# Three merge-gate tiles on blocks 0 and 1 between the halves of the first convolved tiles, and the first root written in front

## The chip, the cores and the metric

The kernel runs on one core of one Trainium2 chip. The metric is the device time of one execution, in microseconds (us). Before the change three runs took 3191.61, 3194.91 and 3195.35 us; the median is 3194.91 us. One more execution was taken by the hardware profiler, and all rows quoted below come from it.

## The reference

Two equal layers of an encoder over 2048 tokens with 1024 channels, in float32, and an RMSNorm at the end. One layer, cut to what matters here:

```python
h = rms_norm(x, norm_w)                      # over the 1024 channels of a token
proj = h @ w_in                              # 1024 -> 5648 columns
qkv, z_a, a_lg, b_lg, cf_val, cf_glu, z_b, gate_lg = split(proj)
qkv = silu(depthwise_conv(qkv, width 5))     # branch A: gated DeltaNet, 4 heads
o = gated_delta(q, k, v, g, beta)            # chunked scans, forward and backward
y_a = (rms(o) * dn_norm_w * silu(z_a)) @ w_dn_out
u = depthwise_conv(cf_val * sigmoid(cf_glu), width 31) + cf_conv_b   # branch B
y_b = (silu(layer_norm(u)) * silu(z_b)) @ w_cf_out
gate = sigmoid(gate_lg + gate_b)             # 2 x 1024 columns: the merge gates
x = x + (gate[0] * y_a + gate[1] * y_b) @ w_out
```

## The kernel before

**Tiling.** Channels lie on the partitions, tokens on the free axis. The 2048 tokens are four *blocks* of 512 (blocks 0 and 1 are the first *half*). The normalised input of a block is held as `h` in two parts, a rounded one and its remainder (`split`, L156: ScalarE rounds, VectorE subtracts), and so is every weight tile (`whi`, `wlo`). One *dense tile*, 128 output channels by one block, is 8 steps over the input channels with three matmuls each (L174 whi by hi, L175 whi by lo, L176 wlo by hi), 24 matmuls of 128x512. `weight` (L160) loads a tile in two halves through the raw buffers `wraw` and splits both. There are two buffers each for `wraw`, `whi` and `wlo`.

**Order of the program.** Engines run their queues in order. A scheduler puts the instructions of the first stages into each queue, from the order in which the code issues them, the free buffers, and its own estimates; in the recurrence (`delta`) the written order is kept. The stages of a layer are: per head `conv_tiles` for k and q, then v, then the two conformer projections and two activated tiles; then `gates(0)`, the 16 merge-gate tiles on blocks 0 and 1 (32 dense tiles); then `delta`, the scans; then `merge`.

**Work on the side.** VectorE's long work, the 31-tap convolutions, the triangular solves and the layer norms of the conformer branch, sits in the list `back`, and `pump` releases some of it after every dense tile (L177 to L183). `delta` has short matmuls with long waits between them; dense work for TensorE comes from `filler`: `gates(1)`, the 16 gate tiles on blocks 2 and 3, and then `early_merge`, which computes the branch B product for blocks 0 and 1 (operand `uop`). The filler hands out 8 steps for each of its 32 gate tiles and 4 for each of the 16 products, 320 steps in all; `delta` pulls 304 of them by the constants LEAD, STEP and TAIL, and runs what is left after its last instruction. Where `back` isn't empty after `gates(0)`, the layer pulls filler steps, 8 at a time, until it is (the `while self.back` loop at L375).

**The first normalisation** (`first_norm`, L287) is a generator that advances step by step. For each block it squares and adds up the 8 channel tiles of `x` (`sqa`; block 0 on VectorE, the others on GpSimd) and yields; then it sums over the partitions on TensorE (`token_sum`, L198, into `nv`), takes the inverse square root by nine small VectorE instructions (`rsqrt`, L187) and yields; then it spreads the root over the partitions (`dg`, L208), scales `x` (L327) and splits it into `h`, with a yield after every second channel tile. `need` and `step_lead` advance it from inside `conv_tiles`.

**The first convolved tiles** (`conv_tiles([4, 0], block)`) keep their two weight tiles over both halves. Per block they compute the small projection `wab` (16 matmuls, L408 and L409) and two dense tiles, k and q; after each half they convolve both with 5 taps (one ScalarE instruction, L551, and four VectorE taps, L553) and apply SiLU.

**The hand-over to the merge.** The last chunk pair's scans are transposed on TensorE (L1045), multiplied by the SiLU gate (L1046), stored to `og`, loaded again as `gop` and split; the first dense tiles of `merge` read `gop`.

Of the kernel before, what the change touches and what calls it, by code (L numbers as in the profile page):

```python
# [14 lines left out]
P = 128  # L15
# [4 lines left out]
KD = 8  # L20
# [5 lines left out]
R1 = 3.0  # L26
R3 = 4.5
GAP = 0
SPLIT = 247
LEAD = (8, 10, 6, 6, 6, 4)  # L30
STEP = (4, 4, 4, 4)
# [45 lines left out]
class Trunk:  # L77
# [120 lines left out]
    def token_sum(self, ps, src, n):  # L198
        for i in range(n):
            self.nc.tensor.matmul(ps[:, i:i + 1], src[:, i * P:(i + 1) * P], self.ones[:, 0:1],  # L200
                                  start=True, stop=True)

    def spread(self, ps, r, n):
        dg = self.pst.tile([P, NB], F32, tag="st", name="dg").rearrange("p (a b) -> p a b", b=P)
        for i in range(n):
            self.nc.vector.tensor_scalar(out=dg[:, i, :], in0=self.ident, scalar1=r[:, i:i + 1],
                                         scalar2=None, op0=ALU.mult)
            self.nc.tensor.matmul(ps[:, i * P:(i + 1) * P], self.ones, dg[:, i, :], start=True, stop=True)  # L208
# [39 lines left out]
    def run(self):  # L248
        tc, nc, a = self.tc, self.nc, self.a
        with tc.tile_pool(name="cst", bufs=1) as cst, \  # L250
                tc.tile_pool(name="vec", bufs=1) as self.pv, \
                tc.tile_pool(name="dsc", bufs=1) as self.pds, \
                tc.tile_pool(name="big", bufs=4) as self.pbig, \
                tc.tile_pool(name="mid", bufs=3) as self.pmid, \
                tc.tile_pool(name="hmd", bufs=5) as self.phm, \
                tc.tile_pool(name="stg", bufs=3) as self.pst, \
                tc.tile_pool(name="sml", bufs=14) as self.psm, \
                tc.tile_pool(name="wgt", bufs=2) as self.pw, \
                tc.tile_pool(name="drm", bufs=1, space=DRAM) as drm, \
                tc.tile_pool(name="pdn", bufs=3, space=PSUM) as self.ppd, \  # L260
                tc.tile_pool(name="pzz", bufs=5, space=PSUM) as self.ppz:
            con = cst.tile([P, 4, P], F32, name="con")
            nc.scalar.dma_start(con, a["consts"])
            self.ident = con[:, C_ID, :]
            self.ones = con[:, C_ONE, :]
            self.con = con
            self.sig = cst.tile([P, 1], F32, name="sig")
            nc.gpsimd.memset(self.sig[0:64], 1.0)
            nc.gpsimd.memset(self.sig[64:128], -1.0)
            self.junk = cst.tile([P, P], mybir.dt.bfloat16, name="junk")  # L270
            fnw = cst.tile([P, KD], F32, name="fnw")
            nc.scalar.dma_start(fnw, a["fnorm"])
            self.drm = drm
            xd = None
            self.vec = self.pv.tile([P, NV], F32, tag="vec", name="vec")
            nc.scalar.dma_start(self.vec, a["vecs"][0])
            self.ready = 0
            h = [None] * 4
            self.h = h
            self.scalar_weights(0)  # L280
            self.lead = self.first_norm(a)
            next(self.lead)
            xd = [a["x"][k] for k in range(KD)]
            for l in range(self.depth):
                h, xd = self.layer(l, h, xd, fnw)

    def first_norm(self, a):  # L287
        nc = self.nc
        stage = self.big([P, 2, KD, NB], F32, "x0")
        for blk in range(4):  # L290
            half, b = divmod(blk, 2)
            self.h[blk] = self.big([P, 2, KD, NB], F32R, f"h{blk}")
            hi, lo = self.h[blk][:, 0], self.h[blk][:, 1]
            src = [a["x"][k, :, blk * NB:(blk + 1) * NB] for k in range(KD)]
            if half == 0:
                x = [stage[:, b, k, :] for k in range(KD)]
            elif b == 0:
                x = self.first_tiles()
            if blk < 3:
                for k in range(KD):  # L300
                    self.load(x[k], src[k])
            acc = self.st("sqa")
            eng = nc.gpsimd if blk else nc.vector
            for k in range(KD):
                sq = self.st("sq0") if k else acc
                if blk == 3:
                    self.load(sq, src[k])
                nc.scalar.activation(sq, sq if blk == 3 else x[k], AF.Square)
                if k:
                    eng.tensor_tensor(out=acc, in0=acc, in1=sq, op=ALU.add)  # L310
            yield
            ps = self.pz()
            self.token_sum(ps, acc, 4)
            v = self.sm(4, "nv")
            r = self.sm(4, "nr")
            nc.vector.tensor_scalar(out=v, in0=ps[:, 0:4], scalar1=1.0 / D, scalar2=EPS,
                                    op0=ALU.mult, op1=ALU.add)
            self.rsqrt(r, v, 4)
            yield
            if blk == 3:  # L320
                x = self.first_tiles()
                for k in range(KD):
                    self.load(x[k], src[k])
            pr = self.pz()
            self.spread(pr, r, 4)
            for k in range(KD):
                nc.vector.scalar_tensor_tensor(out=x[k], in0=x[k], scalar=self.vec[:, V_NW + k:V_NW + k + 1], in1=pr,  # L327
                                               op0=ALU.mult, op1=ALU.mult)
                self.split(hi[:, k, :], lo[:, k, :], x[k])
                if k == KD - 1:  # L330
                    self.ready = blk + 1
                if k % 2:
                    yield
# [13 lines left out]
    def layer(self, l, h, xd, fnw):  # L347
        self.l = l
        self.h = h
        self.kq_d = self.drm.tile([NCH, P, H, 2, P], F32, name=f"kq{l}")  # L350
        self.kv_d = self.drm.tile([NCH, P, 2, H, P], F32, name=f"kv{l}")
        self.g_d = self.drm.tile([NCH, P, H, 2, P], F32, name=f"gr{l}")
        self.inv_d = self.drm.tile([H, P, 1024], F32, name=f"inv{l}")
        self.gc_d = self.drm.tile([P, P], F32, name=f"gc{l}")
        self.gs_d = self.drm.tile([P, P], F32, name=f"gs{l}")
        self.bp_d = self.drm.tile([H, 32, P], F32, name=f"bp{l}")
        self.za_d = self.drm.tile([H, P, L], F32, name=f"za{l}")
        self.zb_d = self.drm.tile([4, P, L], F32, name=f"zb{l}")
        self.cv_d = self.drm.tile([4, P, L], F32, name=f"cv{l}")
        self.u_d = self.drm.tile([4, P, L], F32, name=f"u{l}")  # L360
        self.gt_d = self.drm.tile([16, P, L], F32, name=f"gt{l}")
        self.o_d = self.drm.tile([NCH, P, H, P], F32, name=f"o{l}")
        self.og_d = self.drm.tile([H, P, L], F32, name=f"og{l}")
        for j in range(H):
            self.head(j)
            self.conformer(j)
            self.act_tile(24 + j, self.zb_d[j], AF.Silu)
            self.act_tile(12 + j, self.za_d[j], AF.Silu)
        for blk in range(4):
            self.back.append(self.conformer_norm(blk))  # L370
        self.rate = R3
        for _ in self.gates(0):
            pass
        self.fill = self.filler()
        while self.back:  # L375
            for _ in range(KD):
                next(self.fill)
        self.drain()
        self.rate = 0.0
        self.delta()  # L380
        return self.merge(l, xd, fnw)
# [124 lines left out]
    def conv_tiles(self, cols, block=None):  # L506
        nc = self.nc
        self.rate = R1
        ws = [self.weight(self.a["w_in"][self.l, c], KD) for c in cols]
        accs = []  # L510
        prev = [None] * len(cols)
        for half in range(2):
            cur = []
            for i, c in enumerate(cols):
                cur.append(self.padded(half, TAPS, prev[i], "cin") if half or not i else None)
            for b in range(2):
                blk = 2 * half + b
# [4 lines left out]
                for i, c in enumerate(cols):  # L522
                    self.step_lead(2)
                    ps = self.pd()
# [7 lines left out]
            for i, c in enumerate(cols):  # L532
# [4 lines left out]
                n = HALF - 2 if half == 0 else HALF + 2  # L537
# [248 lines left out]
        v_.tensor_tensor(out=cv, in0=cv, in1=zb, op=ALU.mult)  # L786
        self.pstore(self.u_d[:, :, sl].rearrange("j p t -> p j t"), cv)

    def gates(self, half):
        nc = self.nc  # L790
        seq = [(j, b) for j in range(16) for b in range(2)]
        if half:
            seq = seq[:28] + [(14, 0), (15, 0), (14, 1), (15, 1)]
        ws = {}
        for i, (j, b) in enumerate(seq):
# [3 lines left out]
            blk = 2 * half + b  # L799
            ps = self.pd()  # L800
# [11 lines left out]
    def delta(self):  # L812
# [240 lines left out]
        def pull(n):  # L1053
            for _ in range(n):
                if next(fill, GAP) == GAP:
                    return
# [70 lines left out]
    def filler(self):  # L1127
        wcf = self.a["w_cf"][self.l]
        u = None
        for n, v in enumerate(self.gates(1)):  # L1130
# [9 lines left out]
            if n == 31 * KD - 1:  # L1140
                ahead = self.weight(wcf[0], 4)
            if SPLIT <= n < SPLIT + 8:
                b, k = divmod(n - SPLIT, 4)
# [229 lines left out]
```

## Time and profile before

| | |
|---|---|
| median of three runs | 3194.91 us |
| the profiled execution, its own time | 3187.47 us |
| its span on the core | 3185.7 us |
| busy share of the span: TensorE, VectorE, ScalarE, GpSimd | 97%, 75%, 43%, 9% |
| mean granted TensorE clock | 0.993 of full speed |
| TensorE busy in 0 to 50, 50 to 100, 100 to 150 us | 27.81, 40.15, 49.04 us |
| the same in 1200 to 1250, 1250 to 1300 us | 45.77, 46.28 us |

A row of the timeline gives the start in us, the busy time of the row, the engine, the line, the tile written and the tiles read, how many records are merged in it, and in brackets how long the engine had stood idle before it and what released it. A 128x128 or 128x1 matmul in float32 shows two records for one instruction. A row of the waits says who waited for whom, for how long in total, how often, and the longest wait.

### The profile page before, as it was taken

Reading aid. Unit: us, or ns where it says so; the run is one execution under the profiler, and the core shown is the slowest. Engines: PE = TensorE matmul, PEld = TensorE weight load, DVE = VectorE, ACT = ScalarE, POOL = GpSimd, SP = SyncE. Lnnn points to the kernel's source line nnn. Section 1 sums busy time; section 2 is a strip of 40 time slices with the busy share of each in tenths; the row PEclk is TensorE's granted clock in tenths of the full one; section 3 lists DMA queues with packets and bytes.
Section 4 is the critical chain, followed back from the end, with each engine's and each line's share of the span. In section 5 each row is a group of like instructions: output and inputs, shape, how many; then the busy total and the mean of one; then the engine's idle time right before and its main releaser. Section 6 shows DMA issues by size and latency. Waiting matters only on the chain. (4 is left out here: it accounts for less than half of the span.)

```text
span 3185.7 us, 51259 instructions
## 1 busy us (share of the span) xinstructions
PE 3090.6 (97%) x19110; PEld 2705.8 (85%) x19110; DVE 2398.4 (75%) x4409; ACT 1385.3 (43%) x3104; POOL 302.3 (9%) x297
## 2 busy tenths in 40 slices
PE   6999999999999999999999999999999999999997
PEld 5788888888889998787888888888888999878786
DVE  7789898987646697745676989898955567867655
ACT  5625151522444466533345242425234445655332
POOL 3000000000122231000000000000002222200000
PEclk9999999999999999999999999999999999999999
DMA  4323222334687886654413131414357777855634
GB/s 141 90 96 93 87 93 87 93 112 133 206 288 247 258 267 208 198 185 133 135 53 101 66 120 60 120 60 123 117 186 261 243 252 255 283 182 192 204 126 146
DMA packets 427545, 501.70 MB, mean 157 GB/s; under 512 B 96224, under 2 KB 260704, under 8 KB 427296
## 3 DMA queue, kind: packets, MB, share of 16 engines
q1 hardware_dynamic: 354544, 388.58, 39.2%
q10 hardware_dynamic: 64688, 80.09, 7.3%
q0 software_dynamic: 8064, 29.76, 2.5%
q8 instruction: 150, 2.46, 0.3%
q14 instruction: 99, 0.81, 0.1%
HBM read 342.74 MB, written 155.58 MB: 156 GB/s over the span
## 5 line engine op out<-in xcount | busy, mean ns | idle before, releaser
L174 PE MATMUL pd<-h,whi 128*128 128x512 f32 x2816 | 1092.1, 388 | 0.0
L176 PE MATMUL pd<-h,wlo 128*128 128x512 f32 x2816 | 1070.4, 380 | 1.9 <-DVE wlo L158 1.9
L175 PE MATMUL pd<-h,whi 128*128 128x512 f32 x2816 | 1070.9, 380 | 0.0
L728 DVE SCALAR_TENSOR_TENSOR cacc<-gp,vec,cacc 128x1009 f32<-128x1009 f32 (+1 forms) x480 | 614.3, 1280 | 37.5 <-ACT cacc L726 34.3
L176 PEld LDWEIGHTS pd<-h,wlo 128*128 128x128 f32 x2816 | 533.8, 190 | 79.3 <-DVE wlo L158 3.5
L174 PEld LDWEIGHTS pd<-h,whi 128*128 128x128 f32 x2816 | 534.0, 190 | 79.0 <-issue 1.4
L175 PEld LDWEIGHTS pd<-h,whi 128*128 128x128 f32 x2816 | 534.5, 190 | 72.4 <-issue 1.9
L157 ACT ACTIVATE whi<-wraw 128x512 fp32r<-128x512 f32 x400 | 242.7, 623 | 473.2 <-PE pd L175 335.9
L158 DVE TENSOR_TENSOR wlo<-wraw,whi 128x512 fp32r<-128x512 f32 x400 | 275.0, 701 | 142.1 <-ACT whi L157 141.8
L553 DVE SCALAR_TENSOR_TENSOR acc<-cin,vec,acc 128x1022 f32<-128x1022 f32 (+1 forms) x192 | 246.5, 1299 | 14.4 <-ACT acc L551 13.2
L176 PE MATMUL pd<-yhi,wlo 128*128 128x512 f32 x512 | 194.9, 381 | 3.8 <-DVE wlo L158 3.7
L174 PE MATMUL pd<-yhi,whi 128*128 128x512 f32 x512 | 194.6, 380 | 0.9 <-ACT whi L157 0.9
L175 PE MATMUL pd<-ylo,whi 128*128 128x512 f32 x512 | 194.0, 379 | 0.0
L808 ACT ACTIVATE go<-pd,vec 128x512 f32<-128x512 f32 x128 | 87.1, 680 | 147.9 <-PE pd L176 138.2
L529 ACT ACTIVATE cin<-pd 128x512 f32<-128x512 f32 x96 | 57.0, 594 | 154.7 <-PE pd L176 154.6
L176 PEld LDWEIGHTS pd<-yhi,wlo 128*128 128x128 f32 x512 | 96.8, 189 | 19.9 <-DVE wlo L158 6.4
L740 ACT ACTIVATE ao<-pd 128x512 f32<-128x512 f32 x64 | 38.3, 598 | 170.0 <-PE pd L176 169.9
L174 PEld LDWEIGHTS pd<-yhi,whi 128*128 128x128 f32 x512 | 96.8, 189 | 15.4 <-ACT whi L157 2.0
L175 PEld LDWEIGHTS pd<-ylo,whi 128*128 128x128 f32 x512 | 96.8, 189 | 13.6
L174 PE MATMUL pd<-uop,whi 128*128 128x512 f32 x256 | 101.0, 395 | 6.6 <-ACT whi L157 6.5
L176 PE MATMUL pd<-uop,wlo 128*128 128x512 f32 x256 | 99.1, 387 | 2.3 <-DVE wlo L158 1.4
L175 PE MATMUL pd<-gop,whi 128*128 128x512 f32 x256 | 97.7, 381 | 3.0 <-DVE gop L158 3.0
(297 smaller groups left out, 4754.9 us busy)
## 6 DMA issues: line engine op xcount, KB each, us to landing
wraw<-w_in SPq DMA_DIRECT2D x240, 256.0 KB, 3.3
gt<-go ACTq DMA_DIRECT2D x128, 256.0 KB, 3.6
dl<-gr SPq DMA_DIRECT2D x128, 256.0 KB, 5.2
dl<-kq SPq DMA_DIRECT2D x64, 512.0 KB, 6.1
dl<-kv SPq DMA_DIRECT2D x64, 512.0 KB, 5.8
wraw<-w_out SPq DMA_DIRECT2D x96, 256.0 KB, 3.0
kq<-acc SPq DMA_DIRECT2D x16, 1024.0 KB, 5.5
gr<-go ACTq DMA_DIRECT2D x64, 256.0 KB, 2.2
```

Of the source, the lines that this page charges most:

```text
L157: self.nc.scalar.activation(hi, src, AF.Copy)
L158: self.nc.vector.tensor_tensor(out=lo, in0=src, in1=hi.bitcast(F32), op=ALU.subtract)
L174: mm(ps, whi[:, k, :], xhi, start=k == 0, stop=False)
L175: mm(ps, whi[:, k, :], xlo, start=False, stop=False)
L176: mm(ps, wlo[:, k, :], xhi, start=False, stop=k == kk - 1)
L529: nc.scalar.activation(cut(t[:, o + b * NB:o + (b + 1) * NB]), sort(ps), AF.Copy)
L553: self.nc.vector.scalar_tensor_tensor(out=out, in0=t[:, k:k + n], scalar=wc(k), in1=out, op0=ALU.mult, op1=ALU.add)
L728: self.nc.vector.scalar_tensor_tensor(out=acc, in0=t[:, k:k + n], scalar=wc(k), in1=acc, op0=ALU.mult, op1=ALU.add)
L740: nc.scalar.activation(cut(o), sort(ps), func)
L808: nc.scalar.activation(cut(o), sort(ps), AF.Identity, bias=self.vec[:, V_GB + j:V_GB + j + 1])
```

## The change

It touches layer 0 alone. (1) The generator is advanced one step further before the layers start, so that the sum, root and `nv` of block 0 are issued ahead of the first weights. (2) For block 0 the eighth square isn't added on VectorE; four more small matmuls add it in PSUM (`token_add`). (3) Between the halves of the first two convolved tiles the kernel runs gate tiles 0, 1 and 2 on blocks 0 and 1, six dense tiles, with the normalisation of block 3 stepped along with them. Since there are two weight buffers, the weights of k and q are loaded and split again afterwards. (4) `gates(0)` of layer 0 then runs gate tiles 3 to 15, 26 dense tiles instead of 32.

```diff
@@ first lines
+EARLY = 3
@@ Trunk
+    def token_add(self, ps, src, n, first, last):
+        for i in range(n):
+            self.nc.tensor.matmul(ps[:, i:i + 1], src[:, i * P:(i + 1) * P], self.ones[:, 0:1],
+                                  start=first and i == 0, stop=last, skip_group_check=True)
@@ run
             self.lead = self.first_norm(a)
             next(self.lead)
+            next(self.lead)
@@ first_norm
-                if k:
+                if k and (blk or k < KD - 1):
                     eng.tensor_tensor(out=acc, in0=acc, in1=sq, op=ALU.add)
             yield
             ps = self.pz()
-            self.token_sum(ps, acc, 4)
+            if blk:
+                self.token_sum(ps, acc, 4)
+            else:
+                self.token_add(ps, acc, 4, True, False)
+                self.token_add(ps, sq, 4, False, True)
@@ layer
-        for _ in self.gates(0):
+        for _ in self.gates(0, 0 if l else EARLY):
             pass
@@ conv_tiles
         for half in range(2):
             cur = []
+            if half and block and not self.l:
+                for i, _ in enumerate(self.gates(0, 0, EARLY)):
+                    if i % KD == 0:
+                        self.step_lead(2)
+                ws = [self.weight(self.a["w_in"][self.l, c], KD) for c in cols]
@@ gates
-    def gates(self, half):
+    def gates(self, half, first=0, end=16):
         nc = self.nc
-        seq = [(j, b) for j in range(16) for b in range(2)]
+        seq = [(j, b) for j in range(first, end) for b in range(2)]
```

Four places in the engines' queues. The lines of the changed kernel lie 1 to 16 higher than those of before (L159 is the remainder of a split, L327 the `nv` of the root, L569 the tap of a convolution, L1061 and L1062 the transposes and the product of the hand-over).

VectorE at the first root of block 0, before:

```order
L310 TENSOR_TENSOR sqa<-sqa,sq_133 128x512
L310 TENSOR_TENSOR sqa<-sqa,sq_136 128x512
L158 TENSOR_TENSOR wlo<-wraw,whi 128x512 x2
L316 TENSOR_SCALAR nv<-pz 128x4
L190 TENSOR_SCALAR nr<-nv 128x4
L192 TENSOR_SCALAR rsv<-nv 128x4
L194 TENSOR_TENSOR rst<-nr,rsv 128x4
```

VectorE at the same place, changed:

```order
L317 TENSOR_TENSOR sqa<-sqa,sq_133 128x512
L327 TENSOR_SCALAR nv<-pz 128x4
L159 TENSOR_TENSOR wlo<-wraw,whi 128x512
L191 TENSOR_SCALAR nr<-nv 128x4
L193 TENSOR_SCALAR rsv<-nv 128x4
L159 TENSOR_TENSOR wlo<-wraw,whi 128x512
L195 TENSOR_TENSOR rst<-nr,rsv 128x4
```

One add is gone, and the two remainders of the first weight tile now stand behind `nv`, inside the root, where they stood ahead of it.

VectorE around the first half's convolutions, changed (`h_398` is block 2 normalised, `acc` the convolutions, `nv` that of block 3; of the `wlo` rows the first two here belong to gate tile 1, the others to gate tile 2 further on):

```order
L338 SCALAR_TENSOR_TENSOR x0h<-x0h,vec,pz 128x512 x2
L569 SCALAR_TENSOR_TENSOR acc<-cin,vec,acc 128x1022
L159 TENSOR_TENSOR h_398<-x0h,h_398 128x512 x2
L569 SCALAR_TENSOR_TENSOR acc<-cin,vec,acc 128x1022 x6
L159 TENSOR_TENSOR wlo<-wraw,whi 128x512
L569 SCALAR_TENSOR_TENSOR acc<-cin,vec,acc 128x1022
L159 TENSOR_TENSOR wlo<-wraw,whi 128x512
L327 TENSOR_SCALAR nv<-pz 128x4
```

Before, the same rows stand there without the two `wlo` and with the copies for the second half's convolutions in their place. New is that the remainders of gate tile 1's weights stand behind seven of the eight taps.

TensorE in the gate tiles, changed (`h_107` is block 0, `h_234` block 1; ahead of these rows stand the 48 matmuls of gate tile 0, and L201 is the partition sum of block 3):

```order
L175 MATMUL pd<-h_107,whi 128x512
L176 MATMUL pd<-h_107,whi 128x512
L175 MATMUL pd<-h_234,whi 128x512
L176 MATMUL pd<-h_234,whi 128x512
L201 MATMUL pz<-con,sqa 128x1 x4
L177 MATMUL pd<-h_107,wlo 128x512
L175 MATMUL pd<-h_107,whi 128x512
```

None of it stood there before: behind block 1's tiles came the `wab` matmuls of block 2.

TensorE at the hand-over to the merge, before; 44 more rows of `uop` follow these, and then `gop`:

```order
L176 MATMUL pd<-uop,wlo 128x512
L1045 MATMUL pz<-con,dm_6984 128x128 x8
L174 MATMUL pd<-uop,whi 128x512
L175 MATMUL pd<-uop,whi 128x512
L176 MATMUL pd<-uop,wlo 128x512
L174 MATMUL pd<-uop,whi 128x512
```

TensorE at the same place, changed:

```order
L177 MATMUL pd<-uop,wlo 128x512
L1061 MATMUL pz<-con,dm_7083 128x128 x8
L175 MATMUL pd<-gop,whi 128x512 x2
L176 MATMUL pd<-gop,whi 128x512
L177 MATMUL pd<-gop,wlo 128x512
L175 MATMUL pd<-gop,whi 128x512
```

The 48 `uop` matmuls (16 filler steps) that stood between the last transposes and the merge have moved away. By the code they are pulled ahead of the recurrence: with 26 instead of 32 gate tiles one entry of `back`, a conformer layer norm, is left after `gates(0)`, the loop at L375 pulls 16 filler steps until it is done, and of the 320 steps none is left after the 304 pulls of `delta`. In layer 1 nothing of this changes: 16 steps are left there as before.

## The prediction, made before the changed kernel was run

> **What bounds the kernel now.** I read the page's span and busy times first, then busy time by stretches of 50 us, then the waits and the timeline of the stretches where TensorE isn't full.
>
> ```profile
> span 3185.7 us, 51259 instructions
> PE 3090.6 (97%) x19110; PEld 2705.8 (85%) x19110; DVE 2398.4 (75%) x4409; ACT 1385.3 (43%) x3104; POOL 302.3 (9%) x297
> ...
> 0.00:50.00 50.00, 27.81 (x111) 21.94 (x112) 33.39 (x71) 26.54 (x45) 18.65 (x19) 0.97 0.49 167
> 50.00:100.00 50.00, 40.15 (x177) 32.02 (x176) 43.36 (x80) 26.37 (x41) 13.69 (x9) 0.90 0.28 84
> ```
>
> TensorE is busy for 3090.6 of 3185.7 us, so about 95 us can be won at all. Of these 22.2 fall into the first 50 us and 9.9 into the next 50 (first busy column), where the granted clock is also below 1 (0.90, the third number from the end). The change adds almost no TensorE work and takes none away: it moves six dense tiles, 144 matmuls, into the second hole. So the question isn't what the tiles cost, but how much idle time they really replace, and what idle time they leave where they stood.
>
> **The root in front.**
>
> ```profile
> 9.50 3.88 DVE L310 TENSOR_TENSOR sqa<-sqa,sq 128x512 f32<-128x512 f32 x5 [1.02 <-ACT sq L308]
> 13.30 1.28 DVE L158 TENSOR_TENSOR wlo<-wraw,whi 128x512 fp32r<-128x512 f32 x2
> 13.43 1.87 PE L200 MATMUL pz<-con,sqa 128*128 128x1 f32 x8 [13.43 <-DVE sqa L310]
> 15.34 0.16 DVE L316 TENSOR_SCALAR nv<-pz 128x4 f32<-128x4 f32 x1 [0.76 <-PE pz L200]
> 31.20 1.05 PE L200 MATMUL pz<-con,sqa 128*128 128x1 f32 x8 [1.37 <-POOL sqa L310]
> ```
>
> One add of 0.78 us (3.88 / 5) goes, so the sum may start that much earlier, at 12.65. But it is now 16 records instead of 8, and 8 took 1.87 here: 12.65 + 2 x 1.8 = 16.25 against 15.34, 0.9 later. Before, the two remainders (1.28) ran while TensorE summed, which cost nothing; now they stand behind nv, inside the root, 1.2 more. The first root comes 2.1 us **later**. Bounds: 0.8 earlier, if the second group runs as fast as 1.05 and the remainders slip into the root's gaps; 2.5 later. Down the chain part of it is lost again: the adds of block 2 on GpSimd set the next sum, and four matmuls more stand ahead of it. I take **+1** for the end of block 1's tiles.
>
> **The hole between the halves.**
>
> ```profile
> 62.38 0.60 ACT L529 ACTIVATE cin<-pd 128x512 f32<-128x512 f32 x1 [1.21 <-PE pd L176]
> 62.40 1.05 PE L208 MATMUL pz<-dg,con 128*128 128x128 f32 x8
> 63.49 2.07 DVE L327 SCALAR_TENSOR_TENSOR x0m<-x0m,vec,pz 128x512 f32<-128x512 f32 x3 [3.88 <-PE pz L208]
> 68.04 0.38 PE L176 MATMUL pd<-h,wlo 128*128 128x512 f32 x1
> 68.26 0.38 PE L408 MATMUL pd<-h,wab 128*128 128x512 f32 x1
> 72.87 1.71 DVE L553 SCALAR_TENSOR_TENSOR acc<-cin,vec,acc 128x1022 f32<-128x1022 f32 x1
> 76.79 10.28 DVE L553 SCALAR_TENSOR_TENSOR acc<-cin,vec,acc 128x1022 f32<-128x1022 f32 x6
> 82.06 0.43 PE L414 MATMUL pz<-con,ab 32*128 32x32 f32 x4 [2.50 <-ACT ab L411]
> 91.03 2.00 PE L208 MATMUL pz<-dg,con 128*128 128x128 f32 x8 [1.99 <-DVE dg L206]
> 95.97 0.63 PE L409 MATMUL pd<-h,wab 128*128 128x512 f32 x1
> 96.40 0.63 PE L408 MATMUL pd<-h,wab 128*128 128x512 f32 x1
> 110.47 0.38 PE L176 MATMUL pd<-h,wlo 128*128 128x512 f32 x1
> ```
>
> Matmuls follow each other every 0.216 us (68.04 to 68.26), or every 0.43 at the low clock (95.97 to 96.40). Blocks 2 and 3 take 128 of them, 27.6 us, with some 2.4 of sums and transposes; the stretch from 68.26 to 110.7 is 42.4. So 12.4 us are idle or slow, and that is the most the gate tiles can fill.
>
> When are their weights there? Gate tile 0 may overwrite k's weights once block 1's k tile is done (62.38). Its two remainders (1.28) then stand ahead of block 2's scaling, which starts at 64.7 instead of 63.49; TensorE needs them at 68.3. In time. Gate tile 1 takes q's buffer, free at 68.3, and ScalarE rounds it soon after, but on VectorE its remainders stand behind the rest of block 2 and **seven taps** of the first convolutions. The six taps ended at 87.07, now 1.2 later at 88.3, and the remainder is there at 89.0. TensorE is through gate tile 0 at 68.3 + 48 x 0.216 = 78.7, runs the four matmuls that need whi alone and the sum of block 3, and stands at 80.5 before the first wlo of gate tile 1. It waits 8.5 us, and starts slow for about 2. So of the 12.4 us some 10.5 stay: **a gain of 2**. Gate tile 2's weights come under this wait and under gate tile 1.
>
> ```profile
> L808 ACT ACTIVATE go<-pd,vec 128x512 f32<-128x512 f32 x128 | 87.1, 680 | 147.9 <-PE pd L176 138.2
> ...
> wraw<-w_in SPq DMA_DIRECT2D x240, 256.0 KB, 3.3
> ```
>
> The tiles bring along six evacuations (0.68 each on ScalarE) with their stores, and six raw loads of 3.3 us. These are moved, not added; the second evacuation waits behind the first half's SiLU, but three PSUM buffers cover that. In SP's queue the loads of gate tile 1 stand ahead of block 3's squares, which delays GpSimd's adds by a us or two, and their sum isn't wanted before VectorE is through the taps. New is the reload: four loads and, in halves, four roundings and four remainders (4 x 0.64 on VectorE). They stand behind block 3's splits while TensorE has 92 matmuls, 20 us, in front of it; without that cover they would cost 5.
>
> Bounds of the wait:
>
> ```profile
> L553 DVE SCALAR_TENSOR_TENSOR acc<-cin,vec,acc x8: 1280/1285/1287, 108.5 to 118.0; 128x1026 f32<-128x1026 f32 x8
> 83.15 1.65 POOL L310 TENSOR_TENSOR sqa<-sqa,sq 128x512 f32<-128x512 f32 x1 [1.76 <-ACT sq L308]
> ```
>
> The second half's taps take 1.285 each, those of the first half 1.71, while GpSimd adds block 3's squares. With seven at 1.285 the remainder comes 3 us sooner: a gain of 5. In the other direction, if gate tile 2's weights come late too, 8 us of a second wait: a loss of 6. I take the value nearest to the rows of this place, 1.71. The Trainium skill ("SBUF — State Buffer", section "SBUF: two separate sides") says that a VectorE operation with two SBUF inputs and a GpSimd operation exclude each other for a whole instruction; this trace agrees (1.71 against 1.285), and by it alone the taps stay slow only as far as the adds still fall beside them.
>
> **A wait further on.** The scalar stage takes its input from the last `wab` block, which now comes after the gate tiles, and its 40 small VectorE instructions mix with eight taps.
>
> ```profile
> 127.50 0.23 DVE L456 COPY abw<-abw 128x128 f32<-128x128 f32 x1
> 128.76 0.29 DVE L470 COPY abw<-pz 128x128 f32<-128x128 f32 x1 [1.03 <-PE pz L468]
> PE pz L466 <- DVE abw L456: 1.0, 1, 1.0
> ```
>
> TensorE waited 1.0 us for it. Now the chain can't start before block 3's wab, and the taps (8 x 1.285 = 10.3) share VectorE with it to the end: I get 13 us after block 3's tiles, and TensorE has two v tiles (10.4) in front of it. A wait of 2.9, **+1.9**; bounds -1 and +4.
>
> **The hand-over.** Sixteen filler steps are pulled ahead of the recurrence, because 26 gate tiles don't give the last layer norm its turns. None is left at the end of layer 0's recurrence.
>
> ```profile
> 1284.59 2.38 PE L1045 MATMUL pz<-con,dm 128*128 128x128 f32 x8 [1.09 <-ACT dm L1040]
> 1286.73 0.46 PE L174 MATMUL pd<-uop,whi 128*128 128x512 f32 x1
> 1287.58 1.52 DVE L1046 SCALAR_TENSOR_TENSOR dh<-pz,vec,dh 128x512 f32<-128x512 f32 x2 [2.27 <-DMA dh<-za]
> 1288.35 1.15 SPq L148 DMA_DIRECT2D og<-dh  x2
> 1291.16 0.33 SPq L145 DMA_DIRECT2D gop<-og  x1
> 1295.63 1.06 ACT L157 ACTIVATE gop<-gop 128x1024 fp32r<-128x1024 f32 x1 [3.03 <-DMA gop<-og]
> 1297.17 0.38 PE L174 MATMUL pd<-gop,whi 128*128 128x512 f32 x1
> PE pd L175 <- DVE gop L158: 1.6, 3, 0.8
> 1228.75 1.05 PE L967 MATMUL pz<-dh,dl 128*128 128x128 f32 x8
> 1234.92 2.08 PE L967 MATMUL pz<-dh,dl 128*128 128x128 f32 x8 [4.23 <-DVE dh L1046]
> ```
>
> The chain from the last transposes to the first `gop` matmul is product, store, load, rounding: 1286.73 to 1297.17, 10.4 us. Before, the 48 uop matmuls (48 x 0.216 = 10.4) filled exactly this. Now nothing stands there, and the chain itself loses nothing: **+10.4**. The time they take ahead of the recurrence isn't a gain, since TensorE is full there. A restart at low clock adds about 1 (after an idle 4.23, L967 took 2.08 instead of 1.05), and most of it falls beside the 2.6 us that the merge waits for the next splits anyway; four evacuations gone from between the splits give up to 1 back. I take **+10.6**, bounds +6 and +13. The Trainium skill ("TensorE: Matmul & The Clock Gate", Part 1) has the clock halved after an idle window of about 3.4 us until one busy window has passed; the 4.23 agrees, but the idle 1.99 before the slow L208 at 91.03 is shorter, and the 2.50 at 82.06 had no such effect. By that rule both new gaps would restart slow, some 1.7 each, which the sum has within a us.
>
> **The sum**, against the profiled execution's 3187.47: +1 - 2 + 1.9 + 10.6 = **+11.5**, 3199.0. That execution lies 7.4 below the median of 3194.91, so for the runs I say 3194.91 + 11.5 = **3206.4**. A measurement can tell about 0.2%, 6.4 us, from no change.
>
> **Rivals.** *A, not slower: the gate weights are in time.* If the tap chain lets gate tile 1's remainders through by 80.5, the whole hole of 12.4 is filled, and the rest gives +1 + 1.9 + 10.6: together +1.1, 3196. For it: the four weight halves are loaded early. Against it: VectorE's queue is in order, and the row shows six taps ending at 87.07. It decides from a remainder at about 84.5, where the sum falls below 6.4. *B, slower still: the reload bites.* Gate tile 2's and k's weights share ScalarE's queue with block 3's rounding; if each waits for a buffer there, TensorE gets a second gap of 5 to 10 us: 3212 to 3216. *C, the stall before the last step moves.* With the filler 16 steps ahead, the switch to `uop` meets another step of the recurrence.
>
> ```profile
> 1233.52 0.69 DVE L1173 TENSOR_TENSOR y<-pd,g 128x512 f32<-128x512 f32 x1 [1.25 <-ACT g L1167]
> ```
>
> L1046 stood behind this and held TensorE for 4.23. If it vanishes, -4.2 and some -2 of low clock: 3200 alone, and with A 3190, the only sum that I can make faster than before. *D: the root really comes in front*, 0.8 earlier: 3204.
>
> **How the numbers follow.** My forecast (with D) 0.60, its own range 3202 to 3212; A 0.18; B 0.13; C 0.09, in a third of it with A. Faster by over 0.2%: 0.05, from C with A and what I don't see. Within: 0.22, from A, the rest of C, and the forecast's low end. Slower: 0.73. The range 3194 to 3214 takes in A and half of B.
>
> **What the changed profile would show.** Root: nv near 16.3 instead of 15.34. Hole: one wait of TensorE on `wlo` of some 8 us near 80 to 90, behind the taps. Hand-over: an idle of about 10 us before the first gop matmul. What would make me wrong: a wait on wlo below 4 us, or gop matmuls that follow the transposes within 6 us.

## The result, and the profile after

The changed kernel takes 3224.78 us (median of 4 runs, 3219.08 to 3226.24), the kernel before beside it 3193.26 (4 runs, 3190.72 to 3195.35). The ratio is 1.0092, 95% interval 1.008 to 1.0104: slower by 29 us, 25 to 33. The profiled execution took 3219.08 with a span of 3217.3, against 3187.47 and 3185.7: 31.6 more, where 11.5 were forecast. The direction was right, the size far off, and the time lies outside the range.

The page of the changed kernel, span and busy times:

```profile
span 3217.3 us, 51278 instructions
PE 3099.8 (96%) x19118; PEld 2713.1 (84%) x19118; DVE 2401.8 (75%) x4412; ACT 1386.0 (43%) x3108; POOL 304.6 (9%) x297
```

TensorE's idle time (span less busy) grew from 95.1 to 117.5 us, its busy time by 9.2, though only eight matmul records (four tiny matmuls) were added: so 22 us are new waiting, and most of the 9 must be matmuls at a low clock (the mean granted clock fell from 0.993 to 0.989). Where they lie is read from busy time by stretches, of the kernel after:

```profile
50.00:100.00 50.00, 37.71 (x164) 30.34 (x163) 45.83 (x75) 27.69 (x45) 22.02 (x13) 0.86 0.38 121
850.00:900.00 50.00, 47.49 (x231) 40.66 (x230) 31.78 (x58) 19.78 (x32) 4.24 (x5) 1.00 0.69 229
900.00:950.00 50.00, 43.15 (x383) 36.62 (x382) 28.88 (x50) 24.52 (x57) 15.35 (x13) 0.93 0.85 285
1200.00:1250.00 50.00, 44.81 (x466) 40.82 (x465) 40.63 (x109) 36.08 (x110) 12.01 (x10) 0.97 0.90 286
1250.00:1300.00 50.00, 45.58 (x399) 41.02 (x399) 36.40 (x100) 27.78 (x88) 7.12 (x6) 0.93 0.55 156
1300.00:1350.00 50.00, 36.29 (x161) 29.19 (x160) 26.39 (x49) 23.94 (x57) 0.00 (x0) 0.83 0.53 161
```

and of the kernel before, from two of these places:

```profile
850.00:900.00 50.00, 50.00 (x271) 43.75 (x270) 23.11 (x41) 20.31 (x38) 11.84 (x11) 1.00 0.77 259
1300.00:1350.00 50.00, 48.84 (x225) 42.23 (x225) 42.63 (x66) 27.98 (x45) 0.00 (x0) 1.00 0.54 178
```

The hole at 50 to 100 is no smaller: TensorE is busy for 37.71 there, before 40.15. Stretches that were full are not full any more: 850 to 950, where the recurrence starts, and 1300 to 1350, the hand-over; the last steps at 1200 to 1300, which had some idle time before (45.77 and 46.28 busy), have a little more. TensorE's waits of the kernel after, in the stretches 0 to 150, 850 to 960 and 1200 to 1400 (total, count, longest):

```profile
PE pd L175 <- ACT go L824: 7.1, 1, 7.1
PE pz L201 <- POOL sqa L317: 4.0, 3, 2.1
...
PE pz L930 <- DVE dl L921: 6.9, 2, 6.0
PE pz L201 <- DVE lnt L782: 2.5, 2, 1.8
...
PE pd L175 <- ACT gop L158: 11.5, 1, 11.5
PE pz L983 <- DVE dh L1062: 5.2, 1, 5.2
PE pz L983 <- ACT dm L992: 3.9, 1, 3.9
```

(L824 is L808 of before, L930 is L914, L983 is L967, L1062 is L1046.) The 11.5 was forecast. The 6.9 wasn't, and before has no such wait; where the 5.2 and 3.9 are, before had one of 4.2.

**Late by how much, and where.** The same matmul in two traces tells how much later a kernel has come there. Three serve as marks. A: the first transposes of `acc`, behind the scalar stage (152.46 before, 187.19 after, less 31.1 for the 144 moved matmuls that come earlier now). B: the first product `pz<-dh,dh` of the recurrence (903.51 and 926.89, less 10.4 for 48 filler matmuls run ahead). C: the first matmul of `yhi` (1342.31 and 1373.76), before which both have done the same work.

```profile
187.19 0.27 PE L632 MATMUL pz<-acc 128*128 128x128 f32 x1
926.89 0.23 PE L940 MATMUL pz<-dh,dh 32*32 32x32 f32 x4
1373.76 0.38 PE L175 MATMUL pd<-yhi,whi 128*128 128x512 f32 x1
```

So the changed kernel is late by 3.6 at A, 13.0 at B, 31.5 at C and 31.6 at the end. The forecast's terms up to A gave +0.9, from A to B nothing, from B to C +10.6. Two things failed above all: 9.4 us at the recurrence's start that no term had, and 18.4 instead of 10.6 behind it. A smaller one is the 3.6 instead of 0.9 up to A.

### The profile page after: what moved, and what is told of

The parts are those of the page before. It is cut to its first block, busy times and chain, and to the rows that moved or that the text cites. A ratio compares the mean times of both kernels' runs of the same rounds, so it can differ in the third digit from the quotient of the medians.

```text
span 3217.3 us, 51278 instructions
## 1 busy us (share of the span) xinstructions
PE 3099.8 (96%) x19118; PEld 2713.1 (84%) x19118; DVE 2401.8 (75%) x4412; ACT 1386.0 (43%) x3108; POOL 304.6 (9%) x297
## 5 line engine op out<-in xcount | busy, mean ns | idle before, releaser
L159 DVE TENSOR_TENSOR wlo<-wraw,whi 128x512 fp32r<-128x512 f32 x404 | 278.5, 703 | 139.7 <-ACT whi L158 139.5
L569 DVE SCALAR_TENSOR_TENSOR acc<-cin,vec,acc 128x1022 f32<-128x1022 f32 (+1 forms) x192 | 247.3, 1301 | 14.7 <-ACT acc L567 13.6
L824 ACT ACTIVATE go<-pd,vec 128x512 f32<-128x512 f32 x128 | 87.1, 680 | 151.5 <-PE pd L177 138.2
L175 PEld LDWEIGHTS pd<-yhi,whi 128*128 128x128 f32 x512 | 96.8, 189 | 15.4 <-ACT whi L158 2.2
L176 PEld LDWEIGHTS pd<-ylo,whi 128*128 128x128 f32 x512 | 96.8, 189 | 13.6
```

The lines of the kernel that those rows point to most:

```text
L159: self.nc.vector.tensor_tensor(out=lo, in0=src, in1=hi.bitcast(F32), op=ALU.subtract)
L175: mm(ps, whi[:, k, :], xhi, start=k == 0, stop=False)
L176: mm(ps, whi[:, k, :], xlo, start=False, stop=False)
L569: self.nc.vector.scalar_tensor_tensor(out=out, in0=t[:, k:k + n], scalar=wc(k), in1=out, op0=ALU.mult, op1=ALU.add)
L824: nc.scalar.activation(cut(o), sort(ps), AF.Identity, bias=self.vec[:, V_GB + j:V_GB + j + 1])
```

## The experiments

All runs in one table. Late at the marks is that of the one profiled execution, in us against the first profile of the kernel before; at A and B, the moved or pulled matmuls are taken off as above (two tiles are 10.4). Median and ratio are those of the timed runs.

```
run            A     B     C     end    median    ratio to before (95%)
after          3.6  13.0  31.5  31.6   3224.78   1.0092 (1.008, 1.0104)
again_after    4.3  13.8  32.5  36.2   one run   -
again_before   0.7   3.3   3.9   8.3   one run   -
root_only      0.4   3.3   3.2   5.7   3194.61   1.0001 (0.9988, 1.0013)
pull16         0.8   1.8  19.1  23.4   3211.69   1.0057 (1.0042, 1.0072)
pull8          1.1   3.5  11.7  17.1   3200.73   1.0028 (1.0014, 1.0041)
nopull         3.1  13.1  16.9  20.9   3208.22   1.0047 (1.0032, 1.0062)
turns          3.1  14.0  18.3  21.5   3207.93   1.0044 (1.0027, 1.0061)
rate           2.7   8.6  11.0  14.8   3201.66   1.003  (1.0019, 1.0041)
rate_oldroot   4.5   9.7  14.1  20.9   3203.39   1.0036 (1.0025, 1.0047)
hole_w         0.2   6.1  11.2  11.5   3200.53   1.0022 (1.0009, 1.0035)
hole_both      1.1   5.4   6.9   6.5   3203.09   1.003  (1.0018, 1.0041)
early1        -0.1   3.3   9.3   7.2   3197.49   1.0017 (1.0006, 1.0027)
early2         2.2   7.3  11.9  16.9   3203.48   1.0033 (1.0018, 1.0048)
early1_w      -3.4   0.0   4.7  10.8   3202.05   1.003  (1.0021, 1.0039)
```

**again_before, again_after: how far one profile can be trusted.** The same two kernels once more, no edit.

> The kernel before, profiled once more. 'root_only' has the same cover as before and yet was 2.8 us later between the last convolution of the heads and the recurrence. Theory 'spread': a second profile of the unchanged kernel lags the first by 2 to 5 us at the recurrence, with waits on lnt or at the first step that the first one hadn't. Rival: it lies within 1 us of the first at every landmark, and the 2.8 us are the root's.

> The changed kernel, profiled once more. Theory: the wait of 6.0 at the start of the recurrence, those of 5.2 and 3.9 at its last steps and that of 11.5 at the hand-over come again within 1 us each, as their chains are fixed by the order; the 3.65 us up to the scalar stage come again within 1. Rival 'spread': one of them is gone.

The unchanged kernel, profiled again, is 3.3 late at B and 8.3 at the end: the first profile of before was a good one, and layer 1, which is the same code in all of these, adds anything from -2 to +7. So the last column says little, and a difference at B counts from about 3. (The runs of this table were taken on several chips; how much of the spread lies between chips is not known.) The changed kernel comes out as the first time at all three marks. Its waits in the second profile, 850 to 1400:

```profile
PE pd L175 <- ACT gop L158: 11.1, 1, 11.1
PE pz L983 <- DVE dh L1062: 5.2, 1, 5.2
PE pz L930 <- DVE dl L921: 3.9, 2, 3.0
PE pz L983 <- ACT dm L992: 3.9, 1, 3.9
```

All four are there again; that at the start of the recurrence is 3.0 instead of 6.0 long, so the "within 1 us" failed for this one, though from A to B as much is lost as the first time (9.5 and 9.4). Against again_before, the change's own share is about 3 up to A, 7 from A to B and 18 from B to C, 28 in all, which is what the medians say (25 to 33).

**pull16 and pull8: the filler alone.** The kernel before, with no tile moved and 16 (or 8) steps of the filler run ahead:

```
-        while self.back:
-            for _ in range(KD):
-                next(self.fill)
+        for _ in range(0 if l else 2 * KD):
+            next(self.fill)
```

> The kernel before, with 16 steps of the filler run ahead of the recurrence and no tile moved. Theory 'slip': the missing 16 steps cost by themselves all that was seen behind the recurrence's start, some 8 us at its last steps and 11 at the hand-over: about +19, 3206.5; nothing is lost at the recurrence's start, since the last layer norm ends four tiles ahead of it as before. Rival, the prediction's step: only the hand-over, +10.6, 3198.

> The kernel before with 8 steps of the filler (one tile, 5.2 us) run ahead of the recurrence, half of 'pull16'. Theory 'cover tile by tile': the hand-over waits 5 to 6 us instead of 10.5, one of the two new waits at the last steps is there (about 4 more than before): +8 to +11 us, about half of pull16's +18. Rival 'only the last tile counts': nothing at the hand-over, below +4.

TensorE's waits behind 1200 in pull16:

```profile
PE pd L174 <- ACT gop L157: 10.5, 1, 10.5
PE pz L966 <- DVE dh L1045: 5.2, 1, 5.2
PE pz L966 <- ACT dm L975: 3.9, 1, 3.9
```

These are the changed kernel's three waits, without a single moved tile, and from B to C it loses 17.3. In pull8 the hand-over waits 5.4, about half, and the last steps have a wait of 3.9 where before had one of 4.2, of which 0.7 is left:

```profile
PE pd L174 <- ACT gop L157: 5.4, 1, 5.4
PE pz L966 <- ACT dm L975: 3.9, 1, 3.9
```

So cover is lost tile by tile (8.2 from B to C for one tile, 17.3 for two). With two tiles it is lost twice: at the hand-over, where the tiles themselves are missing, and at the last recurrence steps, which now run beside the short `uop` tiles one step earlier. The queues of the changed kernel show what stands in the way there: ScalarE's `dm` (L992), for which TensorE waits 3.9, starts at 1263.38 behind a weight rounding (0.61) and two sigmoids (1.13), and VectorE's product of the hand-over (L1062), for which it waits 5.2, behind a remainder and a product of `y`. At the start of the recurrence pull16 loses nothing (B less A is 1.0).

**nopull, turns, rate: what is left at the recurrence's start.** In `nopull` the loop above is deleted, so the norm's rest is written with no filler around it. `turns` and `rate` let the last norm end inside the 26 gate tiles, `rate` by a faster pump alone, `turns` also with one idle turn less for each block:

```
+R0 = 5.5
...
-Z = '121'
+Z = ('111', '121')
...
-        self.rate = R3
+        self.rate = R3 if l else R0
```

> The changed kernel, but the end of the last layer norm is written without pulling filler. Theory 'slip': last steps and hand-over are as in the kernel before (one wait of 4.2, hand-over filled): -19; at the start of the recurrence the wait stays or grows, from 6.9 to at most 14, since 10.4 us of filler are gone from in front of it: 3200 to 3207. Rival 'the late norm does all of it': the recurrence stays late and the steps behind it too, 3212 to 3219.

> The changed kernel with the pump's turns of layer 0 mended: rate 5.5 instead of 4.5 and one idle turn fewer for each block, so that the last layer norm ends at tile 21 of 26 (before: 27 of 32) and no filler is pulled. Theory 'turns': nine tenths of the loss comes from the six missing turns; what stays is the 3.65 us that the changed kernel loses up to the scalar stage, so 3191 (profiled run), 28 below the changed kernel. Rival 'VectorE is full': the same taps in fewer tiles make TensorE wait in the gate stage, 5 to 15 us: 3196 to 3206.

> The changed kernel with the pump's rate in layer 0's gate stage at 5.5 instead of 4.5, idle turns as they were: the taps end two tiles earlier, the last layer norm at tile 25 of 26, no filler is pulled. Theory 'the norm is a chain': the 10.9 us that 'turns' lost came from the idle turns taken away (its new waits are on lnt), not from the faster taps; so here TensorE loses 0 to 3 us up to the recurrence, and the last steps and the hand-over are as before: profiled run 3191 to 3195. Rival 'VectorE is full': the faster taps cost as much as in 'turns', 3202 to 3208.

In all three B to C falls from 18.4 to between 2.4 and 4.3: with nothing pulled the one wait of 4.2 at the last steps is back and the gap at the hand-over is filled. From A to B `nopull` still loses 10.0, with waits of TensorE of 3.8 on the norm's sums and 3.8 at the recurrence's first products: the late norm costs that without any pulled filler. Its 3208.22 lies just above the range of 'slip' and below that of the rival. The medians lie 18.9 above the kernel before in pull16 and 15.4 in nopull; together that is 34, and the changed kernel's is 31.5, so the two parts account for nearly all of it. `turns` loses as much in another place. Its waits of TensorE from 800 to 950:

```profile
PE pz L777 <- DVE lnt L772: 6.5, 2, 3.7
PE pz L202 <- DVE lnt L783: 1.8, 2, 1.6
```

TensorE waits for the sums of the norm (`lnt`) itself: taking idle turns out only moves the wait. `rate`, with all its turns and the same faster taps, waits 3.5 on `lnt`, as much as again_before, and 1.9 at the first step. So its gate stage shows no new wait, which speaks against "VectorE is full"; but the theory of the chain missed too: the profiled run came out at 3202.96, in the rival's range and not at 3191 to 3195 (median 3201.66), and it loses 5.9 from A to B where again_before loses 2.6.

**early1, early2: fewer tiles.** `EARLY = 1` and `EARLY = 2` in the changed kernel: nothing is pulled, and two tiles or none are left behind the norm, instead of four.

> The changed kernel with EARLY = 1: two gate tiles moved instead of six, the last layer norm at turn 27 of 30, nothing pulled. Theory 'cover': the moved tiles were cover for the chain of the last layer norm, of which the kernel before has four tiles to spare; with two moved, two are left, and the recurrence starts without a new wait. In the hole 10.4 us of tiles meet 12.4 us of idle or slow time; two evacuations fit in the PSUM buffers, so no wait on go: profiled run between 3181 and 3188, the lag at the recurrence below +1. Rival 'the hole is a chain too': block 3's sum comes later by as much as the tiles take, nothing is gained in the hole: 3188 to 3192.

> The same with EARLY = 2: four tiles moved, the last layer norm at turn 27 of 28, nothing pulled. Theory 'cover': no tile is left behind the norm, so a wait of some 3 to 7 us comes at the start of the recurrence, and the last steps and the hand-over stay as in the kernel before: 3190 to 3197. Rival 'pulling alone does it': without pulled filler no new wait at the recurrence, 3184 to 3189.

Both miss: 3197.49 and 3203.48. early2 loses 5.1 from A to B, as "cover" has it, but is also 2.2 late at A. early1 starts the recurrence as late as again_before, within the spread; but the two tiles, 10.4 us, win under 1 us at A. TensorE's waits in its hole:

```profile
PE pz L201 <- POOL sqa L317: 6.8, 1, 6.8
```

"The hole is a chain too" is right for the hole, though not in its time: the tiles run, and then TensorE waits for block 3's sum instead.

**The hole.** `rate_oldroot` is `rate` with the old root. `hole_w` is `rate_oldroot` with the weights of the first two gate columns (and the first step of gate tile 0) written ahead of the taps; `hole_both` also puts block 3's squares behind gate tile 2 and its sum ahead of the last. `early1_w` is `hole_w` with `EARLY = 1` and the old rate.

```
+            if half == 0 and block and not self.l:
+                early = self.gates(0, 0, EARLY)
+                next(early)
             for i, c in enumerate(cols):
...
-                for i, _ in enumerate(self.gates(0, 0, EARLY)):
-                    if i % KD == 0:
-                        self.step_lead(2)
+                for i, _ in enumerate(early, 1):
+                    if i in (2 * KD, 5 * KD):
+                        self.step_lead(1)
```

(The second part is `hole_both`; `hole_w` keeps `step_lead(2)`, once more ahead of the loop.)

> The same as 'rate' with the root as in the kernel before. Theory 'root is absorbed': the 2.5 us by which the first dense tile comes later are waited out again before the scalar stage, as in 'root_only'; so within 1.5 us of 'rate' from there on. Rival 'root adds up': 3 us less than 'rate' at the scalar stage and behind.

> 'rate_oldroot' with the first two gate columns' weights written ahead of the taps of the first halves, nothing else. Theory 'stage buffer': TensorE's wait of 7.1 in the hole is on an evacuation that has no stage buffer, because block 3's squares on GpSimd hold them; so it stays within 2 us, and the time too. Rival, the prediction's 'wlo behind the taps': the wait was due at 82.5 for the remainders as well, and with them early it falls to under 3: 4 to 6 us faster than 'rate_oldroot'.

> 'hole_w', and block 3's squares written behind the second gate tile and its sum ahead of the last. Theory 'stage buffer and taps': both reasons are gone, the wait of 7.1 falls below 1.5 and the low clock behind it goes: 7 to 10 us faster than 'rate_oldroot', so 4 to 8 below the kernel before if 'rate' comes out as its theory says. Rival 'block 3 is late': its scaled tiles come late for the second half, and TensorE waits there instead, 3 to 8 us: no gain.

> 'early1' with the root as in the kernel before and the gate column's weights written ahead of the taps of the first halves. Theory: as 'early1', and no wait for a remainder in the hole: 3178 to 3186, the only version that may come out below the kernel before by more than 0.2 per cent. Rival 'the hole is a chain too': as 'early1', 3187 to 3191.

TensorE's waits from 60 to 150 in rate_oldroot, then in hole_w, then in hole_both:

```profile
PE pz L202 <- POOL sqa L317: 12.1, 1, 12.1
PE pd L178 <- DVE wlo L160: 1.0, 1, 1.0
```

```profile
PE pd L178 <- DVE wlo L160: 2.9, 1, 2.9
PE pz L202 <- POOL sqa L317: 2.5, 1, 2.5
```

```profile
PE pz L202 <- POOL sqa L317: 10.3, 1, 10.3
```

The old root made nothing better (3203.39, 1.7 above `rate`), so "root adds up" is out. But its wait isn't that of `rate`: instead of 7.1 on `go` TensorE waits 12.1 on block 3's sum. So hole_w could not test "stage buffer" as meant. With the weights early the 12.1 fell to 2.5, with 2.9 on a remainder, and the lateness at A fell by 4.3, nearer to the rival than to "stage buffer". In hole_both no evacuation holds TensorE, but the sum comes too late, as its rival had it. early1_w won most at A (4.1 against again_before), and gave it back behind. Single profiles mislead here: those of hole_both and early1_w (3193.9 and 3198.3) lie below the medians of their kernels (3203.09 and 3202.05), and all timed medians lie above before, by 0.2 to 0.4%. No version tried beats the kernel before.

**root_only: the root.** The kernel before with the second step of the norm in front and the last square added by four more sum matmuls (eight in all):

```
             next(self.lead)
+            next(self.lead)
...
-                if k:
+                if k and (blk or k < KD - 1):
...
```

> The kernel before with the root's part alone (second step of the norm in front, the last squares summed by eight more matmuls). Theory 'root': the 3.3 us by which the changed kernel is later after block 1's tiles come from this part, so the profiled run is 3.3 us above that of before, about 3190.8, and the lag at TensorE's 100th dense matmul is 3 to 4 us. Rival, the prediction's term: +1, about 3188.5, the first root 2.1 later and half of that absorbed by the chain behind.

Neither the 3.3 nor the +1 is there: the first dense tile is 2.9 later, and at A nothing of it is left (0.4, again_before 0.7). The ratio is 1.0001.

## Why the forecast came out too low

Two steps of the forecast failed: it priced the place that the tiles were taken from, the recurrence's start, at nothing (9.4 us measured, about 7 against again_before), and its term for the hand-over, 10.6, covered only one of the places that lose the pulled filler (18.4 measured). The gain of 2 in the hole failed as well, and cost less.

**The root: right in its start, nothing at its end.** The scaling of the sum, `nv`, was due at 16.25.

```profile
16.13 0.16 DVE L327 TENSOR_SCALAR nv<-pz 128x4 f32<-128x4 f32 x1 [3.67 <-PE pz L206]
```

It came at 16.13. The first root was to be 2.1 later; the first dense tile is 2.5 later here. The +1 for the chain behind is 0 by root_only, whose first dense tile is 2.9 later: the waits behind the root, on the adds and scaled tiles, absorb it.

**The hole: the wait as forecast, by another path, and no gain.** Rows of VectorE, ScalarE and TensorE in the hole of the kernel after:

```profile
79.82 11.28 DVE L569 SCALAR_TENSOR_TENSOR acc<-cin,vec,acc 128x1022 f32<-128x1022 f32 x6
91.03 1.75 DVE L159 TENSOR_TENSOR wlo<-wraw,whi 128x512 fp32r<-128x512 f32 x1
88.86 0.69 ACT L824 ACTIVATE go<-pd,vec 128x512 f32<-128x512 f32 x1 [2.05 <-POOL sqa L317]
89.61 0.79 PE L175 MATMUL pd<-h,whi 128*128 128x512 f32 x1 [7.08 <-ACT go L824]
92.28 1.87 PE L201 MATMUL pz<-con,sqa 128*128 128x1 f32 x8 [1.46 <-POOL sqa L317]
```

TensorE stopped at 82.53 (89.61 - 7.08; forecast 80.5) until 89.61 (forecast 89.0). The remainder behind the taps was later still, 91.03, so the forecast's reason held too; but TensorE had already stopped earlier, for an evacuation, and that the two times agree so well is luck. "Three PSUM buffers cover that" was the wrong step: the first evacuation (`go`) of the gate tiles stands in ScalarE's queue behind two squares of block 3, for whose loads ScalarE idles 5.15 and 1.52, and then waits itself for a stage buffer, which block 3's squares hold until GpSimd has added them (2.05, in its bracket). This is read from the trace; no run changes the number of stage buffers. hole_w, with the weights early, still waits for a remainder and for the sum, and hole_both, with the squares late, for the sum. Instead of the gain of 2, about 3 were lost up to A, although the scalar stage waited only 0.4 and not 2.9.

**The recurrence's start: the term that was missing.** The forecast said of the pulled steps that "the time they take ahead of the recurrence isn't a gain, since TensorE is full there", and priced that place at nothing. But the moved tiles were themselves the cover there. The last layer norm needs its turns, one for a gate tile; before it ended four tiles ahead of the recurrence, now it ends after the pulled ones, with none. The last product of the last norm, before and after:

```profile
872.49 2.29 DVE L786 TENSOR_TENSOR lnc<-lnc,lnz 128x2048 f32<-128x2048 f32 x1 [2.11 <-ACT lnc L784]
```

```profile
915.94 2.29 DVE L802 TENSOR_TENSOR lnc<-lnc,lnz 128x2048 f32<-128x2048 f32 x1
```

It starts 31.0 us ahead of B before and 10.9 after; in nopull 10.0, in early2 12.1, in `rate` 12.3, in early1 21.5. Rows of SP, ScalarE, VectorE and TensorE of the kernel after:

```profile
SPq L146 <- DMA u<-lnc: 8.0, 1, 8.0
...
896.60 0.80 SPq L146 DMA_DIRECT2D dm<-gc  x2
899.84 1.15 SPq L146 DMA_DIRECT2D wraw<-w_in  x2
908.08 0.63 ACT L158 ACTIVATE whi<-wraw 128x512 fp32r<-128x512 f32 x1 [13.22 <-DMA wraw<-w_in]
908.74 0.69 DVE L159 TENSOR_TENSOR wlo<-wraw,whi 128x512 fp32r<-128x512 f32 x1 [9.42 <-ACT whi L158]
909.35 2.28 DVE L797 TENSOR_TENSOR lnc<-lnc,pz 128x2048 f32<-128x2048 f32 x1
919.01 0.31 PE L930 MATMUL pz<-dh,dl 32*32 32x32 f32 x2 [6.00 <-DVE dl L921]
```

Read from the top: SP's queue holds for 8.0 us until the store of block 2's norm frees a buffer of the recurrence; a filler weight load stands behind it, so ScalarE idles 13.22, VectorE 9.42, and behind that remainder stands the norm's own scaling (L797) and then the recurrence's first products. TensorE waits 6.00. Before, SP's queue is held for a norm's store just as long (8.7 us), but only until 860.90, 43 us ahead of B, and TensorE is full there. The path by the filler's weights is that of the changed kernel alone; but nopull, which has no such load there, keeps the loss (10.0 from A to B), and pull16 does not have it: the late norm costs it, not the pulled filler. With fewer moved tiles it shrinks (early2 5.1, early1 3.4 from A to B, the last not told apart from again_before's 2.6).

**The hand-over: the idle right, the term too small.** Forecast: about 10 us idle before the first `gop` matmul; measured 11.54, and 10.5 in pull16. The +10.6 was a price for this gap alone. pull16 puts the whole at 17.3: the two waits at the last steps (5.2 and 3.9 for 4.2) add 4.9, and most of the rest must be the low clock behind each gap. Rival C had looked at this step, and only asked whether the stall of 4.23 would vanish; it got company instead.

**The chances.** Slower had 0.73, and was right. The range ended at 3214, since its bounds were worked out for the places where something was added, and not for the place from which the tiles were taken.

What stays open: why the versions that pull nothing still take 0.2 to 0.5% more than before. One thing repeats in those with fewer tiles or a faster pump (`rate`, `rate_oldroot`, hole_w, hole_both, early1, early2, early1_w): ScalarE idles 2.4 to 4.7 us for the filler's weights, whose rounding stands in its queue ahead of the `dh` that TensorE needs at B, and TensorE waits 0.9 to 2.6 us for that `dh`. In the two profiles of before ScalarE idles about 1 us there (2.3 in root_only), and TensorE doesn't wait. From B to C these versions lose another 1.5 to 6.0, before 0 and 0.6. Why the weights are late even in early1, and where all of the loss behind B lies, is not shown.

## What to carry to other kernels

A tile that is moved into idle time leaves the place it came from, and there it was the cover of some chain: before pricing the hole, count what chain ran beside those tiles, by how many tiles it ended early, and what is late when they are gone. Filler that runs early is missing at the end, and may cost more there than its own length (here 17.3 us for 10.4), because the steps that it accompanied meet the next stage's work too. A hole that is waiting for a chain of small steps (here loads, squares and adds of one block) is filled only as far as that chain doesn't share buffers and queues with the filling: six tiles won nothing here, and two won 4.1 us at best (early1_w at A), which the kernel did not keep.

## What was unexpected of the hardware

The same wait of 2.11 us ahead of L201 had two prices. Rows of the kernel after, and of its second profile, with the stretch behind (granted clock is the third number from the end):

```profile
58.77 1.05 PE L201 MATMUL pz<-con,sqa 128*128 128x1 f32 x8 [2.11 <-POOL sqa L317]
58.80:62.20 3.40, 3.40 (x20) 3.11 (x21) 3.24 (x11) 0.74 (x2) 0.00 (x0) 1.00 0.28 77
```

```profile
56.95 1.05 PE L201 MATMUL pz<-con,sqa 128*128 128x1 f32 x8 [2.11 <-POOL sqa L317]
58.80:62.20 3.40, 3.40 (x9) 2.70 (x8) 2.97 (x16) 0.00 (x0) 0.00 (x0) 0.50 0.29 77
```

Once the clock stayed at 1.00; once it was 0.50 for 3.4 us, from 1.8 us behind the end of the wait on, with 9 matmul records instead of 20. So the same short wait cost nothing in one profile and some 1.7 us (half of the 3.4) in the other, which may be part of the spread between profiles. The Trainium skill ("TensorE: Matmul & The Clock Gate", Part 1) says that the window which decides is free-running, so that the same kernel starts cold for a different time in each run; this pair agrees. By the same part of the Trainium skill the clock falls after an idle window of about 3.4 us. The idle stretch ahead of the low clock was shorter here, 2.11 us; which window the chip counted isn't shown. Behind the long waits the low clock cost more than the forecast's "about 1" to "about 2" had it:

```profile
85.30:98.90 13.60, 7.84 (x22) 6.12 (x23) 13.07 (x25) 7.18 (x9) 4.56 (x3) 0.50 0.53 170
1317.50:1334.50 17.00, 5.43 (x13) 3.65 (x13) 6.94 (x7) 5.79 (x7) 0.00 (x0) 0.50 0.81 256
```

Behind the wait of 7.08 the clock stayed at 0.50 for 13.6 us, 9.3 of them after TensorE had restarted at 89.61, with a second wait (1.46) in between. At half the clock the 7.84 busy us there cost some 3.9 us, and the 5.43 at the hand-over some 2.7.
